# Stick-breaking attention with running products against differences of values, and subtracts and copies moved between engines, in one layer of a hybrid trunk on one Trainium2 core

## The chip, the cores and the metric

The kernel runs on one core of one Trainium2 chip. [...] The metric is the device time of one execution in microseconds (us), lower is better. Matrix products write to PSUM, eight banks of 128 partitions x 512 floats; everything else lies in SBUF.

## The reference, cut to what matters

One layer with a prompt of 2048 tokens and a sample of 32 tokens: RMSNorm, one projection, stick-breaking attention in 8 heads of 64 next to an RWKV-7 recurrence in 8 heads of 64, an output projection, and a SwiGLU block. All of it is in float32. The part that the change touches is the attention:

```python
z = jnp.einsum('bqhd,bkhd->bhqk', q, k) / math.sqrt(SB_HEAD_DIM)
mask = k_pos[None, :] < q_pos[:, None]
log_1mb = jnp.where(mask, jax.nn.log_sigmoid(-z), 0.0)
after = lax.cumsum(log_1mb, axis=3, reverse=True) - log_1mb
weight = jnp.where(mask, jnp.exp(jax.nn.log_sigmoid(z) + after), 0.0)
o = jnp.einsum('bhqk,bkhd->bqhd', weight, v)
```

So the weight of key s for query t is sigmoid(z[t,s]) times the product of sigmoid(-z[t,j]) over all keys j between s and t. With R[t,s], the product of sigmoid(-z[t,j]) over j from s up to t-1, the same weight is R[t,s+1] - R[t,s].

The recurrence keeps a 64 x 64 state per head and is done in chunks of 64 tokens (33 chunks with the sample).

## The kernel before

Products of float32 numbers are made from halves: a number is rounded to the format float32r (the upper half, "h"), the remainder is kept as the lower half ("l"), and a product is hh + hl + lh. The helper split (lines 102 to 104) makes both halves: ACT casts, then DVE, or the engine named, subtracts.

Three stages follow each other. **Projection** (superblock, to line 676): three blocks of 640, 768 and 640 tokens, in each 27 groups of 128 columns of w_in. A group is 48 matmuls on PE (colgroup, line 323), then its own work on ACT, DVE and POOL, part of it deferred by one or more groups (defer). The group "va" (g_va, lines 638 to 659) makes the attention's values for two heads: vq keeps them by columns, fin turns them to rows by token (tok_major, line 307), stores them, splits them (lines 656 and 657) and writes the halves to vhl_d in DRAM.

**Attention, recurrence, and the output projection of the first 1024 rows** run interleaved: three Python generators yield weights, and the one that is furthest behind goes next (line 1132). attention() makes two lists: A holds the scores of one block of 128 queries against up to 512 keys; B holds a turn and the values for 128 keys of such a block against up to 512 queries. In each step it gives one entry of A, one turn that is at least LAG = 4 steps behind its scores, and the values LAG2 = 2 steps after their turn. For 8 heads and 4 groups of 512 queries (qg), key blocks (kc) run from qg down to 0; kc == qg is the diagonal, where blocks are 128 to 512 wide. That makes 320 scores and 320 turns. Their steps:

- scores: two matmuls into a bank z (lines 794, 795; three banks, psZ), on the diagonal a third that adds -2^100 to the masked part (797). Then stick: ACT makes R = sigmoid(-z/8) (line 754) and b = sigmoid(z/8) (755), DVE runs the product backwards over the keys in place (757), POOL multiplies b by R shifted by one key (758). R goes on from one key block to the next; for this POOL copies or sets one column (787, 800).
- turn: up to four PE transposes of b into a bank wt (line 809; two banks, psW), and split into wth (ACT, line 103) and wtl (DVE, line 104).
- values: two matmuls that add to av (lines 823, 824), at the end of a query group ob and oT to DRAM (828 to 830).

The recurrence takes for each chunk: up (PE 1057) and its copy Us (DVE 1059), sap (PE 1067) and VS (ACT 1068), snp (PE 1076), the sum (DVE 1081) and its product with the decays PC (DVE 1083), yp (PE 1089, 1091) and Yt (ACT 1094); beside it, for the next chunk, M (DVE 1015) and TTt (ACT 1026).

**Output projection of the rest, and SwiGLU** (from line 1146) run on PE without a gap worth naming; the change does not touch them.

The order on each engine comes from the framework's scheduler, which goes through the program by priority and places an instruction where it expects its inputs and its buffer to be ready; at run time every engine keeps that order and waits by semaphores. A tile that shares a tag with others takes one of the tag's buffers and waits until it is free.

Of the kernel before, what the change touches and what calls it, by code (L numbers as in the profile page):

```python
# [17 lines left out]
P = 128  # L18
# [34 lines left out]
def kernel(ctx: ExitStack, tc: tile.TileContext, x_prompt, x_sample, cache_k, cache_v,  # L53
# [17 lines left out]
    vhl_d = [dp.tile([TP, 2, P], F32, name=f"vhl_d{c}") for c in range(4)]  # L71
    QR_d = dp.tile([NCH + 1, 4, P, P], F32, name="QR_d")
# [40 lines left out]
    with tc.tile_pool(name="pa0", bufs=1) as pe, tc.tile_pool(name="pa1", bufs=1) as pa, \  # L113
# [37 lines left out]
        R_MU, R_ST, R_W0, R_A0, R_KK, R_KA, R_RK = 0, 15, 30, 34, 38, 42, 46  # L151
# [110 lines left out]
        def superblock(sb, T0, NTILE):  # L262
# [375 lines left out]
            def g_va(w, c):  # L638
# [5 lines left out]

                def fin():
# [6 lines left out]
                    if sb == 0:  # L652
                        SP.dma_start(sv[:, c * P:(c + 1) * P], vt[0:TS, NTILE, :])
                    vs = pr.tile([P, 6, 2, P], F32R, tag="hl6", name="vs", bufs=1)
                    v4 = vt[:, 0:NTILE, :].rearrange("p j (h d) -> p j h d", d=HD)
                    ACT.copy(vs[:, 0:NTILE, :, 0:64], v4)
                    DVE.tensor_tensor(vs[:, 0:NTILE, :, 64:128], v4, f32(vs[:, 0:NTILE, :, 0:64]), ALU.subtract)
                    SP.dma_start(vhl_d[c][T0:T0 + NP].rearrange("(j t) h e -> t j h e", t=P),
                                 f32(vs[:, 0:NTILE]))
# [81 lines left out]
    with tc.tile_pool(reuse_waits="tile", name="bp", bufs=6) as bp, \  # L741
# [8 lines left out]
        NB, LAG, LAG2, RW = 10, 4, 2, PAST + TS + 1  # L750

        def stick(z, R, b, k0, n):

# [12 lines left out]
        def load(h, kc):  # L766
            k = bp.tile([P, 512], F32R, tag="k", name="k", bufs=5)
            queue(h).dma_start(f32(k), khl_d[h // 2][h % 2].rearrange("l d t -> (l d) t")[:, kc * 512:(kc + 1) * 512])
            v = bp.tile([P, 4, P], F32R, tag="vp", name="vp", bufs=5)
            queue(h).dma_start(f32(v), vhl_d[h // 2][kc * 512:(kc + 1) * 512, h % 2, :].rearrange("(j p) e -> p j e", p=P))  # L770
            pieces[h, kc] = [k, v]

        def scores(h, qg, kc, j):

            if kc == qg and j == 0:
                q = bp.tile([P, 2, 512], F32R, tag="q", name="q", bufs=3)
                cs = slice(qg * 512, (qg + 1) * 512)
                queue(h).dma_start(f32(q[:, 0]), qhl_d[h // 2][h % 2].rearrange("l d t -> (l d) t")[:, cs])
                for l in range(2):
                    queue(h).dma_start(f32(q[64 - 64 * l:128 - 64 * l, 1]), qhl_d[h // 2][h % 2, l, :, cs])  # L780
                state[h, qg] = q
            if j == 0 and (kc == qg or (qg == 2 and kc < 2)):
                load(h, kc)
# [571 lines left out]
```

## Time and profile before

| | us |
|---|---|
| median of 3 runs | 3561.26 (3555.72 to 3566.15) |
| profiled execution, its own time | 3553.88 |
| its span, first to last instruction | 3551.9 |
| projection | 0 to 911 |
| attention, recurrence, first rows | 911 to 1897 |
| rest of the output projection | 1897 to 2015 |
| SwiGLU | 2015 to 3552 |

The limits of the stages are the first matmul of scores (911.08) and the end of the last values and recurrence (about 1897). To read the page: the busy share of an engine is a mean over stages; a busy PE counts its pipeline's tail, too, so a PE at 88% is not at its peak, and the column PEld beside it is the firmer one. [...]

### The profile page before, as it was taken

Reading aid. Unit: us, or ns where it says so; the run is one execution under the profiler, and the core shown is the slowest. Engines: PE = TensorE matmul, PEld = TensorE weight load, DVE = VectorE, ACT = ScalarE, POOL = GpSimd, SP = SyncE. Lnnn points to the kernel's source line nnn. Section 1 sums busy time; section 2 is a strip of 40 time slices with the busy share of each in tenths; the row PEclk is TensorE's granted clock in tenths of the full one; section 3 lists DMA queues with packets and bytes.
Section 4 is the critical chain, followed back from the end, with each engine's and each line's share of the span. In section 5 each row is a group of like instructions: output and inputs, shape, how many; then the busy total and the mean of one; then the engine's idle time right before and its main releaser. Section 6 shows DMA issues by size and latency. Waiting matters only on the chain.

```text
span 3551.9 us, 51561 instructions
## 1 busy us (share of the span) xinstructions
PE 3348.1 (94%) x20217; PEld 2888.5 (81%) x20217; DVE 1875.3 (53%) x2437; ACT 1265.8 (36%) x2419; POOL 1299.2 (37%) x1207
## 2 busy tenths in 40 slices
PE   8999999989788889998998999999999999999998
PEld 7988898879566677776777899989998888888887
DVE  4665757668876788988884332232222412212213
ACT  6444343443444566665563321111111311111111
POOL 3322433243444576657664322211221222122121
PEclk9999999999787899998999999999999999999999
DMA  5545655566644555554554341111111511111111
GB/s 150 162 145 152 201 147 151 181 172 182 198 117 114 133 148 142 150 139 127 154 138 137 118 132 48 48 36 48 48 48 36 167 60 48 48 48 48 48 42 48
DMA packets 480362, 395.81 MB, mean 111 GB/s; under 512 B 70820, under 2 KB 402160, under 8 KB 480120
## 3 DMA queue, kind: packets, MB, share of 16 engines
q1 hardware_dynamic: 391672, 346.51, 34.1%
q10 hardware_dynamic: 88448, 46.01, 4.8%
q8 instruction: 159, 2.61, 0.3%
q14 instruction: 83, 0.68, 0.1%
HBM read 278.16 MB, written 114.28 MB: 110 GB/s over the span
## 4 chain that ended last, share of the span: by engine, by line
PE 74%; DVE 14%; issue 4%; POOL 3%; ACT 2%; DMA 2%; SPq 0%; ACTq 0%; POOLq 0%; DVEq 0%
PE gu L1268 28%; PE dn L1288 14%; PE mm L323 12%; DVE R L757 5%; PE mo L738 4%; PE wt L809 2%; DVE wtl L104 2%; DVE t L541 1%; DVE Ti L543 1%; PE av L823 1%; PE a4ps L504 1%; PE av L824 1%; PE z L794 1%; PE sap L1067 1%; PE snp L1076 1%
## 5 line engine op out<-in xcount | busy, mean ns | idle before, releaser
L758 POOL TENSOR_TENSOR b<-b,R 128x512 f32<-128x512 f32 (+2 forms) x320 | 394.4, 1238 | 271.9 <-DVE R L757 174.1
L757 DVE TENSOR_TENSOR_SCAN R<-R 128x512 f32<-128x512 f32 (+2 forms) x320 | 440.9, 1387 | 40.0 <-ACT R L754 36.8
L1291 DVE TENSOR_TENSOR x<-x,dn 128x512 f32<-128x512 f32 x374 | 255.6, 687 | 243.4 <-PE dn L1288 243.4
L1268 PE MATMUL gu<-h2h,wh 128*128 128x352 f32 (+1 forms) x1760 | 368.3, 351 | 1.7 <-ACT wh L103 1.2
L1268 PE MATMUL gu<-h2h,wl 128*128 128x352 f32 (+1 forms) x1760 | 369.0, 351 | 0.0
L1268 PE MATMUL gu<-h2l,wh 128*128 128x352 f32 (+1 forms) x1760 | 367.3, 351 | 0.0
L1268 PEld LDWEIGHTS gu<-h2h,wh 128*128 128x128 f32 x1760 | 305.0, 188 | 33.9 <-ACT wh L103 1.4
L1268 PEld LDWEIGHTS gu<-h2l,wh 128*128 128x128 f32 x1760 | 305.3, 188 | 31.0
L1268 PEld LDWEIGHTS gu<-h2h,wl 128*128 128x128 f32 x1760 | 305.1, 188 | 30.2
L1288 PE MATMUL dn<-dh,hdh 128*128 128x512 f32 x748 | 295.1, 394 | 0.0
L1288 PE MATMUL dn<-dh,hdl 128*128 128x512 f32 x748 | 295.0, 394 | 0.0
L1288 PE MATMUL dn<-dl,hdh 128*128 128x512 f32 x748 | 293.8, 393 | 0.0
L809 PE MATMUL wt<-ident,b 128*128 128x128 f32 x1088 | 203.6, 300 | 87.5 <-DVE wtl L104 67.5
L809 PEld LDWEIGHTS wt<-ident,b 128*128 128x128 f32 x1088 | 137.2, 150 | 144.1 <-DVE wtl L104 68.9
L323 PE MATMUL mm<-hh,wh 128*128 128x384 f32 (+4 forms) x1296 | 248.2, 335 | 5.8 <-DVE qhl L614 2.0
L323 PE MATMUL mm<-hh,wl 128*128 128x384 f32 (+4 forms) x1296 | 234.6, 324 | 0.0
L323 PE MATMUL mm<-hl,wh 128*128 128x384 f32 (+4 forms) x1296 | 231.9, 321 | 0.0
L754 ACT ACTIVATE R<-z 128x512 f32<-128x512 f32 (+2 forms) x320 | 174.5, 545 | 142.3 <-PE z L795 69.2
L323 PEld LDWEIGHTS mm<-hh,wh 128*128 128x128 f32 (+1 forms) x1296 | 212.7, 194 | 13.1 <-DVE qhl L614 2.3
L103 ACT CAST wth<-wt 128x512 fp32r<-128x512 f32 (+1 forms) x320 | 169.7, 533 | 135.2 <-PE wt L809 124.7
L323 PEld LDWEIGHTS mm<-hh,wl 128*128 128x128 f32 (+1 forms) x1296 | 211.2, 190 | 2.6
L104 DVE TENSOR_TENSOR wtl<-wt,wth 128x512 fp32r<-128x512 f32 (+1 forms) x320 | 188.7, 595 | 41.3 <-ACT wth L103 38.4
(752 smaller groups left out, 5899.3 us busy)
## 6 DMA issues: line engine op xcount, KB each, us to landing
wraw<-in_w_in ACTq DMA_DIRECT2D x77, 512.0 KB
rawg<-in_w_gate SPq DMA_DIRECT2D x44, 512.0 KB
rawu<-in_w_up SPq DMA_DIRECT2D x44, 512.0 KB
rawd<-in_w_down SPq DMA_DIRECT2D x44, 512.0 KB
A_d<-a SPq DMA_DIRECT2D x28, 512.0 KB
mx<-mixT_d SPq DMA_DIRECT2D x27, 512.0 KB
k<-khl_d SPq DMA_DIRECT2D x42, 256.0 KB
vp<-vhl_d SPq DMA_DIRECT2D x42, 256.0 KB
```

What stands on the lines that cost most here:

```text
L103: ACT.copy(hi, src)
L104: (eng or DVE).tensor_tensor(lo, src, f32(hi), ALU.subtract)
L323: PE.matmul(ps[0:wd, 0:s1 - s0], a_[:, kt, 0:wd], b_[:, kt, s0:s1], start=i == 0, stop=i == 3 * KT - 1)
L504: PE.matmul(ps[:, j, :], KB[64 * e:64 * e + 64, j0 + j, :], QR[64 * e:64 * e + 64, j0 + j, :], start=True, stop=True)
L738: PE.matmul(ps[0:n], a_[:, kt, 0:n], b_[:, kt, :], start=j + kt == 0, stop=j == 2 and kt == KT - 1)
L754: ACT.activation(R[:, k0:k0 + n], z[:, 0:n], AF.Sigmoid, scale=-0.125)
L757: DVE.tensor_tensor_scan(rv, rv, rv, R[:, k0 + n:k0 + n + 1], ALU.mult, ALU.bypass)
L758: POOL.tensor_tensor(b[:, 0:n], b[:, 0:n], R[:, k0 + 1:k0 + n + 1], ALU.mult)
L809: PE.transpose(pt[:, j * P:(j + 1) * P], state[h, qg, kc, j][:, kb * P:(kb + 1) * P], ident)
L1268: PE.matmul(ps[:, 0:n], a_[:, kt, :], b_[:, kt, s0:s1], start=i == 0, stop=i == 23)
L1288: PE.matmul(ps[0:n], a_[:, i * P:i * P + n], b_[:, ds_], start=k == 0, stop=k == 3 * len(js) - 1)
L1291: DVE.tensor_tensor(x1[:n, ds_], x1[:n, ds_], ps[0:n], ALU.add)
```

## The change

1. g_va makes dv, the difference of each value and the one ahead of it in time, on POOL, keeps the last column of a block for the next one in a column of cols, transposes dv on PE beside the values (line 665 of the new kernel) and splits the result out of PSUM; tiles "vs" now come from the tag r4, dv from hl6 (one buffer). The last but one value of each block of 128 tokens is split and stored, too (ve).
2. stick keeps R alone: one sigmoid, one backward product whose second operand is z in PSUM (it is bypassed) and whose start is the first column of the next key block's R. b, its multiply on POOL, and the one-column copies are gone. R is a tile of 512 in 12 buffers. The sample's scores keep the old form (s_stick).
3. values multiplies the turned R by dv. On the diagonal each 128 keys have two matmuls of their own against vd, which is dv with its last row replaced by ve; the rest of the width follows in two more.
4. In a turn with odd kb, ACT copies wt a second time (wf) and POOL subtracts, in place of DVE.
5. Loads of q, k, values and vd are issued ahead of the scores, up to LOOK = 8 steps.
6. In the recurrence ACT makes the copies M and Us, and POOL the product with PC.

```diff
@@ g_va
+                dv = pr.tile([P, 2, MX], F32, tag="hl6", name="dv", bufs=1)[:, 0]
+                pv_ = cols[:, R_PV + c:R_PV + c + 1]
+                POOL.tensor_tensor(dv[:, 0:1], pv_, vq[:, 0:1], ALU.subtract)
+                POOL.tensor_tensor(dv[:, 1:NP], vq[:, 0:NP - 1], vq[:, 1:NP], ALU.subtract)
+                ACT.copy(pv_, vq[:, NP - 1:NP])
...
-                    ACT.copy(vs[:, 0:NTILE, :, 0:64], v4)
-                    DVE.tensor_tensor(vs[:, 0:NTILE, :, 64:128], v4, f32(vs[:, 0:NTILE, :, 0:64]), ALU.subtract)
+                    for q0 in range(0, NTILE, 4):
+                        pt = psT.tile([P, 4, P], F32, tag="tr", name="pdv")
...
+                            PE.transpose(pt[:, i, :], dv[:, (q0 + i) * P:(q0 + i + 1) * P], ident)
+                        vs = r4("vs").bitcast(F32R).rearrange("p (j h e) -> p j h e", j=4, h=2)
+                        split(vs[:, 0:m, :, 0:64], vs[:, 0:m, :, 64:128],
...
+                    PE.transpose(pe_[0:NTILE, 0:P], vq[:, 0:NP].rearrange("p (j t) -> p j t", t=P)[:, :, P - 2], ident)
...
+                    SP.dma_start(ve_d[c, T0 // P:T0 // P + NTILE], f32(ve[0:NTILE]))
@@ attention
-        NB, LAG, LAG2, RW = 10, 4, 2, PAST + TS + 1
+        NB, LAG, LAG2, LOOK, RW = 12, 4, 2, 8, PAST + TS + 1
+        def stick(z, R, n, before):
+            ACT.activation(R[:, 0:n], z[:, 0:n], AF.Sigmoid, scale=-0.125)
+            rv = R[:, 0:n][:, ::-1]
+            DVE.tensor_tensor_scan(rv, rv, z[:, 0:n], before, ALU.mult, ALU.bypass)
...
+                vd = bp.tile([P, 4, P], F32R, tag="vd", name="vd", bufs=3)
+                dma(f32(vd[0:P - 1]), src[0:P - 1])
+                dma(f32(vd[P - 1:P]), ve_d[h // 2, 4 * qg:4 * qg + 4, h % 2, :].unsqueeze(0))
...
-            if kc % 2 and kc < qg:
-                POOL.tensor_copy(R[:, 1024:1025], R[:, 0:1])
-            stick(z, R, b, (kc % 2) * 512, n)
+            R = bk.tile([P, 512], F32, tag="R", name="R", bufs=NB)
+            stick(z, R, n, 1.0 if kc == qg else state[h, qg, kc + 1, j][:, 0:1])
...
-            split(wh[:, c0:], wl[:, c0:], pt[:, c0:])
+            if kb % 2:
+                wf = bq.tile([P, 512], F32, tag="wf", name="wf", bufs=3)
+                ACT.copy(wh[:, c0:], pt[:, c0:])
+                ACT.copy(wf[:, c0:], pt[:, c0:])
+                POOL.tensor_tensor(wl[:, c0:], wf[:, c0:], f32(wh[:, c0:]), ALU.subtract)
+            else:
+                split(wh[:, c0:], wl[:, c0:], pt[:, c0:])
...
+            if kc == qg:
+                vd = state[h, qg, "vd"]
+                for i, w_ in enumerate((wh, wl)):
+                    PE.matmul(av[:, c0:c0 + P], vd[:, kb, :], w_[:, c0:c0 + P], start=kb + i == 0,
+                              stop=qg == 0 and kb == 3 and i == 1)
+                c0 += P
+            if c0 < 512:
+                PE.matmul(av[:, c0:], v[:, kb, :], wh[:, c0:], start=False, stop=False)
+                PE.matmul(av[:, c0:], v[:, kb, :], wl[:, c0:], start=False, stop=kc == 0 and kb == 3)
@@ recurrence
-                DVE.tensor_copy(M[96:128], mp[96:128, 0:256].rearrange("p (h t) -> p h t", h=H))
+                ACT.copy(M[96:128], mp[96:128, 0:256].rearrange("p (h t) -> p h t", h=H))
-                DVE.tensor_copy(Us[up_], up[up_])
+                ACT.copy(Us[up_], up[up_])
-                DVE.tensor_tensor(s3, s3, PC[up_, ch, :].unsqueeze(2).to_broadcast([64, H, 64]), ALU.mult)
+                POOL.tensor_tensor(s3, s3, PC[up_, ch, :].unsqueeze(2).to_broadcast([64, H, 64]), ALU.mult)
```

What this does to the order shows at three places. The first is PE in the projection's second block, behind the transposes of the values of group va; mm are the next group's products, pdv the transposes of the differences, pve that of ve. Before:

```order
L495 MATMUL ptk<-ident,KB 128x128 x4
L504 MATMUL a4ps<-QR,KB 128x128 x8
L307 MATMUL ptok<-ident,vq 128x128 x6
L323 MATMUL mm<-hh_3003,wh 128x384 x8
L323 MATMUL mm<-hh_3003,wl 128x384 x8
```

Now, on the same engine at the same place:

```order
L308 MATMUL ptok<-ident,vq 128x128 x6
L665 MATMUL pdv<-ident,dv 128x128 x4
L324 MATMUL mm<-hh_3071,wh 128x384
L665 MATMUL pdv<-ident,dv 128x128 x2
L324 MATMUL mm<-hh_3071,wh 128x384
L673 MATMUL pve<-ident,vq 6x128
L324 MATMUL mm<-hh_3071,wh 128x384 x6
```

Seven transposes have come in between the values' own and the next group's products, two of those products among them. The second place is DVE in the middle of the attention; R is the backward product, wtl the lower half of a turned block, VST the recurrence's state. Before:

```order
L757 SCALAR_TENSOR_TENSOR R<-R 128x512
L104 TENSOR_TENSOR wtl<-wt,wth 128x512
L757 SCALAR_TENSOR_TENSOR R<-R 128x512
L1081 TENSOR_TENSOR VST<-snp,VST 64x512
L104 TENSOR_TENSOR wtl<-wt,wth 128x512
L1083 TENSOR_TENSOR VST<-VST,PC 64x512
L757 SCALAR_TENSOR_TENSOR R<-R 128x512
```

Now, on DVE in the same stretch of work:

```order
L105 TENSOR_TENSOR wtl<-wt,wth 128x512
L774 SCALAR_TENSOR_TENSOR R<-R,z 128x512 x2
L105 TENSOR_TENSOR wtl<-wt,wth 128x512
L774 SCALAR_TENSOR_TENSOR R<-R,z 128x512 x2
L105 TENSOR_TENSOR wtl<-wt,wth 128x512
L774 SCALAR_TENSOR_TENSOR R<-R,z 128x512
L1123 TENSOR_TENSOR VST<-snp,VST 64x512
```

One subtract now stands to two backward products, which read z, and the product with PC has left. The third place is POOL in the attention; b is the weight that was multiplied there. Before:

```order
L758 TENSOR_TENSOR b<-b,R 128x384
L758 TENSOR_TENSOR b<-b,R 128x512 x2
L800 COPY R<-R 128x1
L758 TENSOR_TENSOR b<-b,R 128x512
L800 COPY R<-R 128x1
```

Now, on POOL; mx is the lower half of an input of the output projection:

```order
L843 TENSOR_TENSOR wtl<-wf,wth 128x512 x2
L1033 MEMSET TTt 32x512
L843 TENSOR_TENSOR wtl<-wf,wth 128x512
L1125 TENSOR_TENSOR VST<-VST,PC 64x512
L843 TENSOR_TENSOR wtl<-wf,wth 128x512
L743 TENSOR_TENSOR mx<-mx,mh 128x1024
```

The multiplies ahead of the transposes are gone; in their place stand subtracts behind every second turn, and the recurrence's product, between POOL's other work.

## Rows read from the trace of the kernel before

**Rows 1.** Stages: length, then busy us of PE, PEld, DVE, ACT, POOL; clock, DMA.

```profile
core 0: us, PE busy (x) PEld busy (x) DVE busy (x) ACT busy (x) POOL busy (x), PEclk, DMA share, GB/s
911.00:1250.00 339.00, 274.48 (x1949) 216.98 (x1949) 246.20 (x325) 169.32 (x384) 178.58 (x213) 0.78 0.50 133
...
1550.00:1897.00 347.00, 318.82 (x2615) 251.89 (x2614) 297.87 (x321) 205.90 (x408) 230.08 (x216) 0.97 0.51 134
911.00:1897.00 986.00, 868.80 (x6862) 689.92 (x6863) 806.69 (x935) 561.22 (x1167) 608.19 (x635) 0.90 0.52 136
0.00:911.00 911.00, 842.13 (x5241) 786.50 (x5241) 614.23 (x879) 388.37 (x779) 299.96 (x290) 0.96 0.58 167
...
2015.00:3552.00 1537.00, 1525.48 (x7596) 1324.67 (x7596) 417.31 (x575) 281.87 (x424) 346.89 (x248) 1.00 0.20 62
```

**Rows 2.** Chain of waits from 911 to 1897 us, shares by line.

```profile
by line: DVE R L757 16.7%; issue 8.4%; PE wt L809 8.2%; DVE wtl L104 5.8%; PE mo L738 5.5%; PE av L823 4.7%; PE av L824 4.3%; PE z L794 3.9%; PE sap L1067 3.5%; PE snp L1076 3.2%; PE z L795 3.0%; POOL b L758 2.7%; PE up L1057 2.1%; PE yp L1
```

**Rows 3.** Groups, 911 to 1897 us: busy us, mean ns, idle before by releaser.

```profile
L757 DVE TENSOR_TENSOR_SCAN R<-R 128x512 f32<-128x512 f32 x224 | 356.9, 1599 | 21.4 <-ACT R L754 19.3 <-POOL R L800 0.3
L758 POOL TENSOR_TENSOR b<-b,R 128x512 f32<-128x512 f32 x224 | 296.4, 1328 | 176.5 <-DVE R L757 116.2 <-ACT b L755 17.7 <-ACT R L754 11.8
L809 PE MATMUL wt<-ident,b 128*128 128x128 f32 x1088 | 203.6, 300 | 87.5 <-DVE wtl L104 67.5 <-POOL b L758 19.1
L104 DVE TENSOR_TENSOR wtl<-wt,wth 128x512 fp32r<-128x512 f32 x224 | 150.6, 677 | 35.2 <-ACT wth L103 33.1
L754 ACT ACTIVATE R<-z 128x512 f32<-128x512 f32 x224 | 137.2, 613 | 93.2 <-PE z L795 69.2 <-PE z L797 14.4 <-POOL b L758 6.8
...
L755 ACT ACTIVATE b<-z 128x512 f32<-128x512 f32 x224 | 136.8, 611 | 2.3 <-PE wt L809 2.2
L103 ACT CAST wth<-wt 128x512 fp32r<-128x512 f32 x224 | 133.3, 598 | 101.6 <-PE wt L809 91.3 <-DMA k<-khl_d 7.2 <-DVE VST L1081 2.2
...
L794 PE MATMUL z<-k,q 128*128 128x512 f32 x224 | 102.4, 457 | 7.2 <-ACT b L755 5.9 <-DMA k<-khl_d 1.3
...
L1083 DVE TENSOR_TENSOR VST<-VST,PC 64x512 f32<-64x512 f32 x31 | 35.7, 1151 | 1.0
...
L1059 DVE COPY Us<-up 64x512 f32<-64x512 f32 x33 | 22.9, 695 | 9.3 <-PE up L1057 8.3
L951 POOL TENSOR_TENSOR Yt<-Yt,gl 128x512 f32<-128x512 f32 x15 | 22.9, 1527 | 2.9 <-DVE Yt L949 1.7 <-ACT b L755 0.9
...
L1015 DVE COPY M<-mps 32x256 f32<-32x256 f32 x32 | 13.8, 430 | 10.5 <-PE mps L1013 9.6
```

**Rows 4.** Single lines, 911 to 1897 us: duration ns min/median/max, first and last start.

```profile
L757 DVE TENSOR_TENSOR_SCAN R<-R x320: 446/1284/3324, 921.3 to 1880.6; 128x512 f32<-128x512 f32 x96, 128x128 f32<-128x128 f32 x32, 128x384 f32<-128x384 f32 x32
...
L104 DVE TENSOR_TENSOR wtl<-wt,wth x320: 258/660/694, 932.8 to 1891.8; 128x512 fp32r<-128x512 f32 x128, 128x256 fp32r<-128x256 f32 x32
...
L1083 DVE TENSOR_TENSOR VST<-VST,PC x31: 689/803/2908, 1049.8 to 1874.8; 64x512 f32<-64x512 f32 x31
```

**Rows 5.** PE in order of time, end of the projection: start us, us, instructions.

```profile
840.71 1.55 PE L323 MATMUL mm<-hh,wh 128*128 128x384 f32 x8
842.11 1.55 PE L323 MATMUL mm<-hh,wl 128*128 128x384 f32 x8
...
852.15 0.71 PE L307 MATMUL ptok<-ident,qf 128*128 128x128 f32 x5
852.61 1.20 PE L323 MATMUL mm<-hh,wh 128*128 128x256 f32 x8
```

**Rows 6.** Groups, 0 to 911 us, columns as in rows 3.

```profile
L344 POOL TENSOR_TENSOR df<-xp 128x640 f32<-128x640 f32 x14 | 18.8, 1340 | 35.4 <-ACT xp L335 31.3 <-ACT kbt L497 2.7 <-DVE rr L346 1.4
...
L307 PE MATMUL ptok<-ident,vq 128*128 128x128 f32 x64 | 11.8, 321 | 1.6 <-DVE kt__8881 L309 1.6
...
L657 DVE TENSOR_TENSOR vs<-vt,vs 128x768 fp32r<-128x768 f32 x4 | 6.0, 1512 | 1.8 <-ACT vs L656 1.8
...
L656 ACT CAST vs<-vt 128x640 fp32r<-128x640 f32 x7 | 5.1, 730 | 14.1 <-DVE vt L309 10.1 <-DMA qhl_d<-qhl 2.2 <-DMA A_d<-a 1.8
```

More of the change, by code (lines that the diff above doesn't have):

```diff
@@ L764, in queue, with load @@
             return ACT if h == 0 else SP
[L766 to L775, printed above, removed]
+        def load(h, qg, kc):
+            dma = queue(h).dma_start
+            if kc == qg:
@@ L776, in scores @@
                 q = bp.tile([P, 2, 512], F32R, tag="q", name="q", bufs=3)
                 cs = slice(qg * 512, (qg + 1) * 512)
-                queue(h).dma_start(f32(q[:, 0]), qhl_d[h // 2][h % 2].rearrange("l d t -> (l d) t")[:, cs])
+                dma(f32(q[:, 0]), qhl_d[h // 2][h % 2].rearrange("l d t -> (l d) t")[:, cs])
                 for l in range(2):
-                    queue(h).dma_start(f32(q[64 - 64 * l:128 - 64 * l, 1]), qhl_d[h // 2][h % 2, l, :, cs])
+                    dma(f32(q[64 - 64 * l:128 - 64 * l, 1]), qhl_d[h // 2][h % 2, l, :, cs])
@@ L781, in scores @@
                 state[h, qg] = q
-            if j == 0 and (kc == qg or (qg == 2 and kc < 2)):
-                load(h, kc)
-            if kc == qg:
-                R = bk.tile([P, RW], F32, tag="R", name="R")
-                e = (qg % 2) * 512 + (j + 1) * P
-                POOL.memset(R[:, e:e + 1], 1.0)
-                state[h, qg, "R", j] = R
-            R = state[h, qg, "R", j]
+            if kc < qg and not (qg == 2 and kc < 2):
+                return
+            k = bp.tile([P, 512], F32R, tag="k", name="k", bufs=6)
@@ new lines, in load @@
+            dma(f32(k), khl_d[h // 2][h % 2].rearrange("l d t -> (l d) t")[:, kc * 512:(kc + 1) * 512])
+            src = vhl_d[h // 2][kc * 512:(kc + 1) * 512, h % 2, :].rearrange("(j p) e -> p j e", p=P)
+            v = bp.tile([P, 4, P], F32R, tag="vp", name="vp", bufs=6)
+            dma(f32(v), src)
+            pieces[h, kc] = [k, v]
+            if kc == qg:
+                vd = bp.tile([P, 4, P], F32R, tag="vd", name="vd", bufs=3)
+                dma(f32(vd[0:P - 1]), src[0:P - 1])
+                dma(f32(vd[P - 1:P]), ve_d[h // 2, 4 * qg:4 * qg + 4, h % 2, :].unsqueeze(0))
+                state[h, qg, "vd"] = vd
@@ L790, in scores @@
+        def scores(h, qg, kc, j):
             k = pieces[h, kc][0]
@@ L822, in values @@
             av = state[h, qg, "o"]
-            PE.matmul(av[:, c0:], v[:, kb, :], wh[:, c0:], start=kc == qg and kb == 0, stop=False)
-            PE.matmul(av[:, c0:], v[:, kb, :], wl[:, c0:], start=False, stop=kc == 0 and kb == 3)
+            if kc == qg:
+                vd = state[h, qg, "vd"]
[6 more added lines that the diff above has]
+                PE.matmul(av[:, c0:], v[:, kb, :], wl[:, c0:], start=False, stop=kc == 0 and kb == 3)
             if kc == 0 and kb == 3:
@@ L894, in attention @@
         def attention():
-            A, B = [], []
+            A, B, loads = [], [], []
             for hq, h in [(hq, h) for hq in range(2) for h in range(H)]:
@@ L905, in attention @@
                     for kc in range(qg, -1, -1):
+                        loads.append((len(A), h, qg, kc))
                         for j in range(4):
@@ L916, in attention @@
                 w = 0.0
+                while loads and loads[0][0] <= t + LOOK:
+                    load(*loads.pop(0)[1:])
                 if t < len(A):
```

27 lines of the change are left out of this document (16 added, 11 removed).

## The prediction

> **What bounds the kernel now.** I read the stages first [rows 1]. SwiGLU has PE busy for 1525 of 1537 us at full clock; nothing of the change is there. In the projection PE is busy for 842 of 911 us: every matmul added there costs its own time. The middle stage, 911 to 1897 us, is another matter. PE shows 869 of 986 us, but its weight loads, the firmer column, only 690 (70%), while DVE has 807 (82%; 86% in the last third), POOL 608 and ACT 561. So in this stage DVE is nearest to its limit, and PE has room that it can't use, because each block goes PE, ACT, DVE, POOL, PE, ACT, DVE, PE in lists of fixed order. The chain of waits says the same [rows 2]: the backward product (L757) is the largest line, 16.7%, wtl has 5.8%, POOL's multiply 2.7%. And the groups show where PE stands still [rows 3]: ahead of its transposes 67.5 us for wtl and 19.1 us for POOL's b.
>
> The single lines then show something that the means hide [rows 4]. The backward product takes 1284 ns in its median over all widths, and up to 3324; its mean at 512 wide is 1599 [rows 3]. The decay product (L1083) goes from 689 to 2908. Both read two operands from SBUF. wtl, which reads one from PSUM and one from SBUF, stays between 258 and 694. So a DVE instruction of the first kind is drawn out in this stage and one of the second is not, and the change makes the product of the second kind, with z from PSUM.
>
> **The change, part by part.** Sums are against the profiled execution's 3553.9 us; the median of the runs lies 7.4 us above it, which I add at the end. The stage's chain is 986 us, so 1% is 9.9 us.
>
> *POOL's multiply and the second sigmoid go.* On the chain the multiply is 2.7%, 27 us: **-27**. ACT's b ran beside other work; 137 us of ACT's list are free at 512 wide [rows 3], and what takes their place is below.
>
> *The backward product reads z.* There is no row of a product with a PSUM operand. Its ends: as long as now (1599), or undisturbed (1284 at 512 wide; that this is the 512 value follows from 512 being 224 of the 320). wtl against L1083 [rows 4] makes the lower end the nearer one. The line's 16.7% are 165 us, and 1 - 1284/1599 is 20%: **-32**, with 0 as the other end. [...]
>
> *Half of wtl leaves DVE.* 160 of 320 turns. Of the chain's 5.8%, 57 us, half: **-28**. For these turns the bank wt is freed by ACT's second copy (as the cast, 598 ns) in place of DVE's subtract (677), so PE's transposes wait no longer than for the other half, unless ACT is behind. ACT loses about 170 us of b over all widths (137 at 512, 96 narrower ones at less) and takes 160 copies, at most 96, plus Us and M, some 37 [rows 3]: its list gets shorter.
>
> *Us, M and the product with PC leave DVE*: 22.9 + 13.8 + 35.7 = 72 us of its list [rows 3]. DVE's two large lines have 22.5% of the chain (222 us) for 545 or so of its 807 busy us; at that ratio, rounded down to 0.28 because these wait for PE as well, 72 us are **-20**. Ends 0 and -72. POOL's product is bounded by L951, 1527 ns at twice the partitions, against 1151: 0.4 us more in each of 31 chunks, 12 us, beside attention work that fills PE; taken at nothing, 12 as the other end.
>
> *TensorE's clock.* In 911 to 1250 us the mean granted clock is 0.78, against 0.97 in the last third [rows 1]; in that first part PE has 64 us idle, more than twice the share of idle that the last third has. Less waiting there should give some of it back. If PE paced it throughout, 274 x (1 - 0.78/0.97) = 54 us; I take **-12**, about a quarter, with ends 0 and -54.
>
> *PE's additions in the stage.* 192 more matmuls: on the diagonal kb 0 to 2 have four in place of two, 6 x 32 groups. The columns are the same. A transpose of 128 columns follows the next in (852.61 - 852.15)/5 = 92 ns, and a product of 384 columns in (842.11 - 840.71)/8 = 175 ns [rows 5], so 128 of its columns cost 58; the cut costs 92 - 58 = 34 ns each, with the weight load: 7, taken as **+8**; at most 192 x 92 = 18.
>
> *Projection.* 64 transposes of dv at 92 ns are 6 us, 12 of ve 1 to 3. The banks that they take are evacuated by ACT and DVE, which have work of the next group ahead; PE's waits for such a bank are 1.6 us for 64 now [rows 6]. dv has one buffer, shared with the q and k halves, so the group q's ACT cast waits behind va's transposes, and the evacuations behind that cast in ACT's list with it; as a price, the 2.2 and 1.8 us that ACT waited for buffers at L656. Together **+12**, from 4 to 30. POOL's subtract (as L344, 1340 ns, 12 times) stands ahead of the next group's df, which waits for ACT anyway (31 of 35 us); cover gone, 16 us. ACT and DVE split the same width from PSUM as they did from SBUF, where L657 took up to 1512: nothing.
>
> *New waits.* A bank z is now held until DVE's product has read it, not until the second sigmoid: 613 + 1284 against 613 + 611 ns, and DVE's queue. What is behind it is PE's next score, and all of PE's list. Three banks, and a score every 986/320 = 3.1 us: a bank has 9 us, the chain needs 2.5. Taken at nothing; the price is a rival. Loads stand up to eight steps ahead in SP's list, where one that waits for its buffer holds up the recurrence's loads behind it; scores wait 1.3 us for a load today, so neither gain nor loss is counted.
>
> Sum: -27 -32 -28 -20 -12 +8 +12 = -99. 3553.9 - 99 + 7.4 = **3462 us**.
>
> **The rivals.**
>
> *PE paces the stage.* After the change no other engine is near its limit: DVE loses 87 (wtl; 65 of them at 512) + 71 (224 x 0.315) + 72 and comes to about 577 of 986, POOL and ACT to less. PE's loads are then the most, 690 + 12. If they reach the 0.82 that DVE holds today, the stage is 702/0.82 = 856 us, a gain of 130; with the first part's loads at the later clock (217 x (1 - 0.78/0.97) = 43 less) it is 804, a gain of 182. The middle, 156, less 12 for the projection: 3417. For it speaks that the lists get shorter on three engines at once; against it, that a chain through five lists seldom lets the next engine go as far.
>
> *The z banks.* The 67.5 us that PE waits for wtl today come back as waits for z: -99 + 67 = -32, 3529. It decides once DVE is more than 6 us behind its sigmoids; POOL's waits for the product, 116 us in all, show that DVE does fall behind.
>
> *POOL in the path of the values, slower than before.* In odd turns the lower half is ready after 598 + 598 + 1328, not 598 + 677: 1.25 us later in 96 turns, half of that in 64, 160 us. If PE stands for all of it, -99 + 160 = +61: 3622. It decides where PE's list reaches the values sooner than 2.5 us behind the turn, or POOL is that much behind; two steps are 6 us, which speaks against it, and on POOL the mx subtract and the recurrence's product stand between, which speaks for it. [...]
>
> *The product isn't shorter from PSUM*, so that this part doesn't do what it might: -67, 3494; with a product of more than 1599, less.
>
> **How the numbers follow.** The forecast, 3435 to 3490: 0.52. PE paces, 3417: 0.25. z banks, 3529: 0.12. POOL in the path: 0.06. Product not shorter: 0.05. The forecast is the likeliest. The range runs from 3390, most of the way to the 182 of the first rival, to 3535, above the z banks; it leaves out a fifth of the first rival, a third of the second and the third. About 0.3% is what a measurement of this kernel can tell from no change. Faster by more than that: everything but POOL's case and a part of the z banks, 0.91; within it 0.04, slower 0.05.
>
> **What would show it.** In the profile after: the middle stage at 870 to 910 us; DVE at about 65% of it; the product at 512 wide near 1284 ns with hardly a spread, like wtl; PE's waits for wtl about halved and none on POOL ahead of a transpose; mm's stage 4 to 30 us longer; the recurrence no later. The forecast is wrong if PE's scores wait for z's banks (DVE's product as the releaser), if values wait for POOL's wtl, if the product stays at 1599, or if the projection loses more than 30 us. If PE is over 80% in weight loads, the first rival has it.

## The result, and the profile of the changed kernel

The changed kernel takes **3707.9 us** (median of 4, 3700.4 to 3713.7), the kernel before 3563.7 (median of 4): 1.041 times as long, 95% interval 1.038 to 1.043. The forecast was 3462, with 3390 to 3535 as its range. It was wrong, and on the wrong side: +144 instead of -99. The prediction had given any slowing a chance of 0.05.

The stages of the changed kernel, to be held against [rows 1]: length; busy us, with counts, of PE (matrix products), PEld (their weight loads), DVE (scans and elementwise work), ACT (sigmoids, casts, copies) and POOL (elementwise work); granted clock, the share of its full speed that PE had in the stretch; DMA share; GB/s.

```profile
core 0: us, PE busy (x) PEld busy (x) DVE busy (x) ACT busy (x) POOL busy (x), PEclk, DMA share, GB/s
0.00:911.00 911.00, 847.26 (x5192) 788.20 (x5192) 602.29 (x852) 389.42 (x801) 312.13 (x300) 0.94 0.55 160
911.00:1410.00 499.00, 328.55 (x2365) 273.45 (x2365) 217.17 (x316) 173.64 (x387) 95.51 (x107) 0.72 0.43 117
1410.00:2060.00 650.00, 589.70 (x4845) 477.09 (x4845) 370.94 (x419) 358.67 (x702) 270.41 (x227) 0.95 0.55 141
2060.00:3705.00 1645.00, 1631.29 (x8089) 1407.32 (x8089) 449.53 (x617) 314.49 (x471) 387.53 (x279) 1.00 0.21 66
```

The loss is in the middle stage. The last product of the values starts at 2046 us instead of 1892, and in the first part, to 1410 us, every engine is idle much of the time, PE for 170 of 499 us, at a granted clock of 0.72. DVE, the fullest engine of the stage before, has 588 us here for 807. So work did leave DVE, and something else came to set the pace. The chain of waits, 940 to 1990 us, shares by line, says what (compare [rows 2]):

```profile
by line: SPq L813 14.2%; DMA vd<-vhl_d 7.5%; PE wt L835 5.7%; PE mo L756 5.3%; DMA ABc<-A_d 4.7%; ACTq L813 4.4%; PE z L822 4.2%; PE z L823 3.3%; DMA mx<-mixT_d 2.9%; issue 2.8%; PE av L862 2.7%; PE av L863 2.7%; PE snp L1118 2.6%; PE sap L
```

SPq and ACTq are the lists of SP and ACT while they issue DMAs. The scan, 16.7% before, isn't among the lines that the row has room for. In its place stand the issue of line 813, the load of the single row into vd, and ahead of it the load of vd's other 127 rows (L812), with its wait. The issues themselves, as ns minimum/median/maximum and first and last start:

```profile
L812 SPq DMA_DIRECT2D vd<-vhl_d x28: 239/362/425, 975.6 to 1966.3; - x28
L812 ACTq DMA_DIRECT2D vd<-vhl_d x4: 246/495/785, 953.3 to 1332.4; - x4
L813 SPq DMA_DIRECT2D vd<-ve_d x28: 618/12686/24127, 975.9 to 1967.0; - x28
L813 ACTq DMA_DIRECT2D vd<-ve_d x4: 12933/16497/20235, 954.7 to 1333.7; - x4
```

The 127 rows are issued in 0.36 us; the DMA behind them stands 12.7 us in the list in its median. It isn't slow by itself: its minimum is 618 ns, in the one of its 28 issues on SP ahead of which other DMAs had come in between, and then the first of those stood, for 10.07 us. SP's list in order of time (start us, duration us), once as it mostly goes and once with another DMA next:

```profile
1150.58 0.25 SPq L812 DMA_DIRECT2D vd<-vhl_d  x1
1150.88 12.51 SPq L813 DMA_DIRECT2D vd<-ve_d  x1
1163.43 0.47 SPq L1027 DMA_DIRECT2D ABc<-A_d  x1
...
1377.22 0.36 SPq L812 DMA_DIRECT2D vd<-vhl_d  x1
1379.98 10.07 SPq L1022 DMA_DIRECT2D QAc<-QR_d  x1
...
1392.81 0.62 SPq L813 DMA_DIRECT2D vd<-ve_d  x1
```

What the DMA engines do meanwhile is in 40 slices of 0.75 us from 1150 us on (busy tenths, then GB/s):

```profile
DMA  9996200000000000000389820237658996101001
GB/s 313 195 234 126 60 18 21 20 21 20 20 21 20 20 21 20 20 21 23 102 294 208 148 40 22 32 82 150 202 137 281 243 289 193 36 22 44 22 22 33
```

Ahead of and behind the load the engines move up to 313 GB/s, during it a steady 20, with the mean busy share of the 16 engines under a tenth (0.07 from 1155 to 1162 us; 16 x 0.07 = 1.1, about one engine's time). The load has 127 x 4 x 512 = 260,096 bytes; at 20.5 GB/s that is 12.7 us, the median of the row above. So these rows go at about a tenth of the rate around them, and SP issues nothing until they are nearly through. Behind it stand the recurrence's loads (ABc, QAc, TTt) and the attention's next ones; on ACT's list, which holds four of these loads, the sigmoids stand behind it too: the first one starts at 995.6 us, behind two such issues of 13.6 and 20.2 us.

Why such a load goes at one engine's share, 20 GB/s, isn't shown: the trace doesn't say which engine moves what. That the following issue stands is shown by the rows of L813.

The groups that answer to [rows 3], 911 to 2050 us (busy us, mean ns, idle before by releaser):

```profile
L774 DVE TENSOR_TENSOR_SCAN R<-R,z 128x512 f32<-128x512 f32 x224 | 280.9, 1263 | 167.7 <-ACT R L772 167.0
L835 PE MATMUL wt<-ident,R 128*128 128x128 f32 x1088 | 197.6, 295 | 21.4 <-DVE wtl L105 19.9 <-ACT wf L842 1.3
L843 POOL TENSOR_TENSOR wtl<-wf,wth 128x512 fp32r<-128x512 f32 x96 | 124.2, 1294 | 214.8 <-ACT wf L842 198.6 <-PE z L825 3.8 <-issue 3.7
L822 PE MATMUL z<-k,q 128*128 128x512 f32 x224 | 106.8, 477 | 61.4 <-DVE R L774 61.4
L1101 ACT COPY Us<-up 64x512 f32<-64x512 f32 x33 | 19.2, 582 | 43.5 <-PE up L1099 43.2
```

Two of the steps are there as forecast: the scan at 512 wide is 1263 ns for 1599, and PE waits 21.4 us ahead of its transposes where it waited 87.5. And one that was taken at nothing: PE's scores wait 61 us for a bank z that the scan still holds.

### The profile page after: what moved, and what is told of

It is laid out like the page before. It is cut to its first block, busy times and chain, and to the rows that moved or that the text cites. A ratio compares the mean times of both kernels' runs of the same rounds, so it can differ in the third digit from the quotient of the medians.

```text
span 3705.9 us, 51315 instructions
## 1 busy us (share of the span) xinstructions
PE 3396.8 (92%) x20485; PEld 2946.1 (79%) x20485; DVE 1639.9 (44%) x2203; ACT 1236.2 (33%) x2360; POOL 1065.6 (29%) x912
## 4 chain that ended last, share of the span: by engine, by line
PE 66%; DMA 9%; DVE 8%; SPq 6%; issue 4%; POOL 3%; ACT 2%; ACTq 1%; POOLq 0%; DVEq 0%
PE gu L1310 27%; PE dn L1330 14%; PE mm L324 7%; PE mo L756 4%; SPq L813 4%; DMA vd<-vhl_d 2%; PE wt L835 2%; DMA ABc<-A_d 1%; DVE t L542 1%; PE z L822 1%; ACTq L813 1%; DVE Ti L544 1%; DMA mx<-mixT_d 1%; PE z L823 1%; DMA wraw<-in_w_in 1%
## 5 line engine op out<-in xcount | busy, mean ns | idle before, releaser
L774 DVE TENSOR_TENSOR_SCAN R<-R,z 128x512 f32<-128x512 f32 (+2 forms) x320 | 344.8, 1088 | 264.6 <-ACT R L772 263.0
L843 POOL TENSOR_TENSOR wtl<-wf,wth 128x512 fp32r<-128x512 f32 (+2 forms) x160 | 171.5, 1073 | 414.2 <-ACT wf L842 357.0
L835 PE MATMUL wt<-ident,R 128*128 128x128 f32 x1088 | 197.6, 295 | 21.4 <-DVE wtl L105 19.9
L822 PE MATMUL z<-k,q 128*128 128x512 f32 (+2 forms) x320 | 143.0, 447 | 79.9 <-DVE R L774 61.8
L324 PEld LDWEIGHTS mm<-hl,wh 128*128 128x128 f32 (+1 forms) x1296 | 209.4, 188 | 2.6
L104 ACT CAST dh<-rawd 128x1024 fp32r<-128x1024 f32 x44 | 44.2, 1047 | 425.5 <-PE dn L1330 424.4
```

The source lines that it names most:

```text
L104: ACT.copy(hi, src)
L324: PE.matmul(ps[0:wd, 0:s1 - s0], a_[:, kt, 0:wd], b_[:, kt, s0:s1], start=i == 0, stop=i == 3 * KT - 1)
L774: DVE.tensor_tensor_scan(rv, rv, z[:, 0:n], before, ALU.mult, ALU.bypass)
L822: PE.matmul(z[:, 0:n], state[h, qg][:, 0, js], k[:, 0:n], start=True, stop=False)
L835: PE.transpose(pt[:, j * P:(j + 1) * P], state[h, qg, kc, j][:, kb * P:(kb + 1) * P], ident)
L843: POOL.tensor_tensor(wl[:, c0:], wf[:, c0:], f32(wh[:, c0:]), ALU.subtract)
```

## The experiments

Theories: **the load** (127 rows at about one engine's share, 20 GB/s, hold what stands behind them in SP's and ACT's lists), against **a slow load of one row**, and, for what is left, **the terms of the sum**. All edits are small; each time is the median, with the ratio to the kernel before and its 95% interval. The kernels were run in several sets, each with its own runs of the kernel before, whose medians lie between 3555.5 and 3567.5 us; a difference of two kernels from different sets is uncertain by some 10 us for that.

**112 + 15 rows instead of 127.** The changed kernel, one line different:

```diff
-                dma(f32(vd[0:P - 1]), src[0:P - 1])
+                dma(f32(vd[0:112]), src[0:112])
+                dma(f32(vd[112:P - 1]), src[112:P - 1])
```

> The changed kernel with one edit: vd's load of 127 rows is issued as 112 rows and 15 rows; the load of the last row (ve) is as it was. Theory A (the load of 127 rows is moved by so few DMA engines that the next DMA on its queue can't be issued for some 13 us, and SP's and ACT's lists stand): the issue after it, L813 in the profile of the changed kernel (median 12.7 us), falls under 1.5 us, the lines SPq, ACTq L813 and DMA vd leave the chain of waits, and the time falls by 150 to 260 us, to 3450 to 3560, near the 3462 forecast. Theory B (the one-row load from ve_d is slow by itself): its issue stays above 10 us and the time within 20 us of 3708. Theory C (loads ahead of the scores hold up the recurrence's loads whatever their rows): the time falls by less than 60 us.

3552.9 us, 1.0004 (0.9985 to 1.0022): 155 us less than the changed kernel (148 when each is held against the kernel before of its own set), for the same bytes in one DMA more. The issues of the three DMAs (112, 15 and 1 rows):

```profile
L812 SPq DMA_DIRECT2D vd<-vhl_d x28: 310/474/1482, 964.6 to 1818.5; - x28
L813 SPq DMA_DIRECT2D vd<-vhl_d x28: 337/498/771, 965.5 to 1819.0; - x28
L814 SPq DMA_DIRECT2D vd<-ve_d x28: 617/626/660, 966.6 to 1819.6; - x28
```

The load of one row, unchanged, is never over 0.66 us now. So the 127 rows are the cause of the loss against before, and the slow single row falls. But the time is that of the kernel before, and 91 us above the forecast: the gain is missing, too.

**The load alone, in the kernel before.** A load of vd that nothing reads, once with 127 + 1 rows, once with 112 + 15 + 1, both from vhl_d:

```diff
+            if kc == qg:
+                vd = bp.tile([P, 4, P], F32R, tag="vd", name="vd", bufs=2)
+                src = vhl_d[h // 2][kc * 512:(kc + 1) * 512, h % 2, :].rearrange("(j p) e -> p j e", p=P)
+                queue(h).dma_start(f32(vd[0:P - 1]), src[0:P - 1])
+                queue(h).dma_start(f32(vd[P - 1:P]), src[P - 1:P])
```

> The kernel before with dead loads added and nothing else: for each of the 32 diagonal blocks a tile vd is loaded in 127 rows and one row, both from vhl_d, in two buffers, and nothing reads it. Theory A: the issue behind each 127-row load takes 10 us or more, and the kernel before gets slower by 80 to 250 us, to 3640 to 3810, though no engine computes anything more. Theory B (ve_d's load) and theory C (the loads' lead): within 30 us of 3563.

> The same dead loads in the kernel before, with the 127 rows issued as 112 and 15; the bytes are the same and there is one issue more. Theory A: no issue above 2 us, the time within 25 us of 3563. If it is the bytes or the number of DMAs that cost, it is as slow as with 127 rows.

127 rows: 3766.4, 1.0599 (1.0573 to 1.0625), and the issue behind the load shows the same picture:

```profile
L776 SPq DMA_DIRECT2D vd<-vhl_d x28: 622/12614/16837, 963.2 to 2029.2; - x28
```

112 rows: 3672.4, 1.0344 (1.0311 to 1.0378). The step from 127 to 112 + 15 is worth 94 us here. But I had expected hardly any cost for what remains, and it is 116 us: loads that nothing reads, of 8 MB in all, aren't free in this stage. Two more kernels ask which part of them it is, with all 128 rows in one DMA, and in two of 112 and 16:

```diff
-                queue(h).dma_start(f32(vd[0:P - 1]), src[0:P - 1])
-                queue(h).dma_start(f32(vd[P - 1:P]), src[P - 1:P])
+                queue(h).dma_start(f32(vd), src)
```

> The kernel before, with a load that nothing reads: all 128 rows of the tile of the diagonal, in one DMA, where 112 + 15 + 1 rows in three cost 116 us and 127 + 1 in two cost 210. Theory 1 (the bytes, 8 MB in the two stretches, delay the loads that the kernel waits for): 3640 to 3680 again. Theory 2 (the small loads of 15 rows and of one row, or the time to issue three, made it): 3556 to 3590.

> The kernel before with the dead load in two DMAs, of 112 and of 16 rows, and none of one row. One DMA of 128 rows cost 31 us, three of 112, 15 and 1 rows 116. Theory 1 (each DMA more costs about the same, by its issue and its small pieces): 3625 to 3645. [...]

One DMA: 3592.0, 1.0090 (1.0071 to 1.0108), 31 us. Two: 3646.7, 1.0243 (1.0208 to 1.0279), 79 us. So one whole load costs about 31, and each further DMA costs more than its own half microsecond of issue in 32 places. What goes with it in the traces is POOL: ahead of clearing a part of TTt, a tile of the recurrence, it waits for the product sap for 27.7 us before, 48.4 with one DMA, 63.0 with two, 98.9 with three, and PE waits for POOL's b ahead of its transposes 19.1, 37.7, 50.0 and 71.4. That fits a recurrence whose loads come later, and a list of POOL in which b stands behind TTt; it is read from the waits and not shown by an experiment. The granted clock of the stretch from 911 to 1890 us goes down beside it, 0.90, 0.90, 0.88 and 0.86; what that costs was not measured.

**No second copy.** With R = 1 at each masked key, the value that row 127 of vd carried can be added once for each block: vp with all its rows in the place of vd, and one product of a row of ones with the block's last value.

```diff
-                dma(f32(vd[0:P - 1]), src[0:P - 1])
-                dma(f32(vd[P - 1:P]), ve_d[h // 2, 4 * qg:4 * qg + 4, h % 2, :].unsqueeze(0))
+                dma(f32(ve), ve_d[h // 2, 4 * qg:4 * qg + 4, h % 2, :].unsqueeze(0))
...
+            PE.matmul(av[:, c0:], v[:, kb, :], wh[:, c0:], start=kc == qg and kb == 0, stop=False)
+            if kc == qg:
+                PE.matmul(av[:, c0:c0 + P], state[h, qg, "ve"][0:1, kb, :], oner, start=False, stop=False)
+            PE.matmul(av[:, c0:], v[:, kb, :], wl[:, c0:], start=False, stop=kc == 0 and kb == 3)
```

> The changed kernel without the second copy of the differences: the diagonal blocks use the tile vp with all its rows, and the last value of each block, which the 127 rows left room for, is added by a product of one row of ones with a tile of one row (4 x 128), 128 columns wide, one per diagonal block. So no load of 127, 112 or 15 rows is left, 8 MB less is loaded, and one small product takes the place of one of two. With 112 + 15 rows the changed kernel took 3553, as the kernel before. Theory 1 (the load of the second copy eats what the rest of the change gains; as dead work beside the kernel before it cost 116): 3430 to 3480. Theory 2 (the rest of the change gains nothing, because TensorE paces the stage and new waits take the place of the old ones; the second copy is hidden once its rows are many enough): 3535 to 3560.

3510.5, 0.9858 (0.9838 to 0.9879): faster than before by 51 us, outside what either theory gave, half of the forecast's gain. Against the kernel with 112 + 15 rows it is 42 us. The tile ve now holds each block's last value, not the last but one.

**Which part of those 42 us.** The copy's loads back as dead loads, with two and with three buffers for ve, and, apart from that, the products in the changed kernel's pieces:

```diff
+                vd = bp.tile([P, 4, P], F32R, tag="vd", name="vd", bufs=2)
+                dma(f32(vd[0:112]), src[0:112])
+                dma(f32(vd[112:P - 1]), src[112:P - 1])
```

```diff
-            PE.matmul(av[:, c0:], v[:, kb, :], wh[:, c0:], start=kc == qg and kb == 0, stop=False)
+            if kc == qg:
+                for i, w_ in enumerate((wh, wl)):
+                    PE.matmul(av[:, c0:c0 + P], v[:, kb, :], w_[:, c0:c0 + P], start=kb + i == 0, stop=False)
```

> e5_no_vd (3510) with the second copy's loads back, in 112 and 15 rows, which nothing reads; its products stay as in e5_no_vd. Theory 1 (of the 42 us between the changed kernel with 112 + 15 rows and e5_no_vd the loads are the cause, by their bytes and by what stands behind them on the lists): 3540 to 3560. Theory 2 (the products in more pieces are the cause): 3505 to 3522.

> e11_dead_loads (3596) with three buffers for ve, as e5_no_vd (3510) has, in place of two. In e11_dead_loads SyncE's list stood 42.8 us in five waits for the products that read an older ve, which neither e5_no_vd nor the changed kernel has. Theory 1 (those waits are in the 85, and the loads alone cost what the changed kernel with 112 + 15 rows loses by them): 3535 to 3560. Theory 2 (the loads alone cost 85, and the changed kernel with 112 + 15 rows hides part of it): 3580 to 3600.

> e5_no_vd (3510) with each diagonal product in the two pieces of the changed kernel, both from vp; no second copy is loaded. There are 192 products more, which the forecast put at 8 us, and at 24 if all stood on the path. Theory 1 (loads): 3508 to 3525. Theory 2 (pieces): 3535 to 3555.

Dead loads: 3595.7, 1.0109 (1.0088 to 1.0130), of which a part was my own doing. With two buffers for ve, SP's list stood at its load (L819) for products that read an older one (us in total, times, longest):

```profile
SPq L819 <- PE av L864: 42.8, 5, 19.8
```

With three buffers that row is down to 10.2 us in three waits (9.2 without the loads, so the expectation was wrong that they have none), and the time is 3583.3, 1.0088 (1.0070 to 1.0106), in the range of the second theory: the loads alone cost 73 us, at 112 + 15 rows still. Pieces: 3529.0, 0.9936 (0.9912 to 0.9960), 18 us, between the ranges of the two theories. By each set's own kernel before the two are 78 and 24. Together 91, more than 42; but the kernel without the copy has 128 small products with ones that the kernel with 112 + 15 rows lacks, and they have 41.8 us of PE's time (327 ns each). 73 + 18 - 42 is 49, near the 42. That they cost all of their busy time is an assumption: no run has taken them out alone.

**The terms of the sum.** First the scan: the kernel with 112 + 15 rows, and the scan's second operand in SBUF again, which also lets the bank z go after the sigmoid.

```diff
-            DVE.tensor_tensor_scan(rv, rv, z[:, 0:n], before, ALU.mult, ALU.bypass)
+            DVE.tensor_tensor_scan(rv, rv, rv, before, ALU.mult, ALU.bypass)
```

> As the run with 112 and 15 rows, and the backward product's bypassed second operand is R itself in SBUF again, not z in PSUM, so that z's bank is free after the sigmoid. If the forecast's term for the product is right (an operand in PSUM keeps POOL's work out of it), the product at 512 wide grows from 1.2 to 1.3 us toward 1.4 to 1.6 us, by POOL's share of now, and the time by 5 to 30 us over the run with 112 and 15 rows. If the banks z that wait for the product cost more than that (PE's scores waited 61.8 us for it in the changed kernel), the time falls by 10 to 50 us.

3598.3, 1.0131 (1.0104 to 1.0158): 45 us slower than with z, more than the 5 to 30 expected. Its groups, and below them the same two with z:

```profile
L774 DVE TENSOR_TENSOR_SCAN R<-R 128x512 f32<-128x512 f32 x224 | 331.6, 1500 | 56.1 <-ACT R L772 55.2
L1126 POOL TENSOR_TENSOR VST<-VST,PC 64x512 f32<-64x512 f32 x31 | 50.4, 1625 | 56.9 <-DVE VST L1124 35.1 <-issue 10.6 <-PE wt L836 4.1
...
L774 DVE TENSOR_TENSOR_SCAN R<-R,z 128x512 f32<-128x512 f32 x224 | 278.6, 1261 | 78.9 <-ACT R L772 78.1
L1126 POOL TENSOR_TENSOR VST<-VST,PC 64x512 f32<-64x512 f32 x31 | 32.3, 1041 | 57.5 <-DVE VST L1124 36.3 <-issue 10.6 <-PE z L826 4.8
```

1500 ns for 1261, and POOL's product with PC 1625 for 1041: as means, instructions of both engines took longer here, where DVE's scan reads both operands from SBUF. Most of their instructions are hardly slower, some much: over all widths the scan has 393/1269/3407 ns as minimum, median and maximum (384/1256/1283 with z), and POOL's product 1039/1159/5287 (1039/1041/1045 with z).

Then, on the kernel without the copy, the lower half of the weights on DVE for every turn, and separately the recurrence's two copies and its product with PC on DVE, as before:

```diff
-            if kb % 2:
-                wf = bq.tile([P, 512], F32, tag="wf", name="wf", bufs=3)
...
-            else:
-                split(wh[:, c0:], wl[:, c0:], pt[:, c0:])
+            split(wh[:, c0:], wl[:, c0:], pt[:, c0:])
```

```diff
-                ACT.copy(Us[up_], up[up_])
+                DVE.tensor_copy(Us[up_], up[up_])
...
-                POOL.tensor_tensor(s3, s3, PC[up_, ch, :].unsqueeze(2).to_broadcast([64, H, 64]), ALU.mult)
+                DVE.tensor_tensor(s3, s3, PC[up_, ch, :].unsqueeze(2).to_broadcast([64, H, 64]), ALU.mult)
```

> As e5_no_vd, but the lower half of the weights is made on VectorE for every turn, as in the kernel before (no tile wf, no subtraction on GpSimd). Theory 1 (the forecast's term of 28 us for the half that left VectorE): 15 to 40 slower than e5_no_vd. Theory 2 (GpSimd's 1.07 us for a tile, after two copies on ScalarE, stands in the path of the values and gives the gain back): from 5 slower to 40 faster than e5_no_vd.

> As e5_no_vd, but the recurrence's two copies (Us and M) and its product with PC are on VectorE, as in the kernel before. Theory 1 (the forecast's term of 20 us for what left VectorE): 10 to 30 slower than e5_no_vd. Theory 2 (the recurrence is a chain of steps that nothing else waits for, VectorE has time to spare, and the product is quicker there): within 10 of e5_no_vd, or faster.

Split on DVE: **3495.7**, 0.9818 (0.9800 to 0.9837), 15 us faster than with half of it on ACT and POOL, and the fastest version of all. Recurrence on DVE: 3514.0, 0.9869 (0.9844 to 0.9894), no difference from 3510.5. The groups of the fastest, 940 to 1850 us:

```profile
L778 DVE TENSOR_TENSOR_SCAN R<-R,z 128x512 f32<-128x512 f32 x224 | 283.0, 1264 | 76.0 <-ACT R L776 75.4
L838 PE MATMUL wt<-ident,R 128*128 128x128 f32 x1088 | 189.4, 284 | 10.8 <-DVE wtl L105 10.3
L105 DVE TENSOR_TENSOR wtl<-wt,wth 128x512 fp32r<-128x512 f32 x224 | 150.5, 673 | 45.6 <-ACT wth L104 45.0
L825 PE MATMUL z<-k,q 128*128 128x512 f32 x224 | 98.9, 441 | 6.8 <-DVE R L778 6.8
```

With all of wtl on DVE, PE waits for it 10.3 us, where it was 67.5 before [rows 3]; with half on POOL it is 8.8, and the values wait 5.7 for POOL's half (8.1 in the weight loads). There was nothing left for the split to gain.

**The start of the stage.** In the fastest version the first values come at 970.6 us and the last at 1832.8; before 933.2 and 1891.9. The stage is 96 us shorter and starts 37 later. Three attempts on the start: ve of the projection in a ring of its own, no loads ahead, and the first with the loads ahead only from the second step.

```diff
-                    ve = pr.tile([P, 256], F32, tag="t2", name="ve").bitcast(F32R).rearrange("p (h e) -> p h e", h=2)
+                    ve = r4("ve")[:, 0:256].bitcast(F32R).rearrange("p (h e) -> p h e", h=2)
...
-        NB, LAG, LAG2, LOOK, RW = 12, 4, 2, 8, PAST + TS + 1
+        NB, LAG, LAG2, LOOK, RW = 12, 4, 2, 0, PAST + TS + 1
...
-                while loads and loads[0][0] <= t + LOOK:
+                while loads and loads[0][0] <= t + (LOOK if t else 0):
```

> As e6_split_dve (3496), but the tile ve of the projection's end lies in the ring r4 and no longer in the buffer t2, which the inverse on VectorE uses step by step. In e6_split_dve the last ve waited 7.9 us for that inverse, ScalarE's list of loads stood behind it, and the first values came 37 us later than in the kernel before (970 against 933). Theory 1 (that wait holds the start): 3483 to 3492. Theory 2 (the start is held by the projection's longer end and by the loads ahead, which keep the DMA engines 0.8 to 0.9 busy from 930 to 990): within 4 of e6_split_dve.

> As e6_split_dve (3496), but without the eight steps ahead (LOOK 0): a load is issued at the step that uses it, as in the kernel before. Theory 1 (the loads ahead crowd the start): 5 to 15 faster, the first values at 950 to 960. Theory 2 (loads ahead spare TensorE waits later, and the start is held by the projection's end): 5 to 40 slower.

> As e8_ve_r4, and the eight steps ahead begin only behind the first step, so that the first loads stand alone. If each of the two holds the start: 3470 to 3487, the first values at 940 to 955. If the projection's longer end holds it: within 5 of e6_split_dve (3496).

3497.1, 3501.4 and 3498.6 (0.9816, 0.9828, 0.9821): none gains, and the first values come later, at 982.8, 976.8 and 988.3 us. The first edit has only exchanged one wait for another: ACT's cast of ve waited 9.2 us for the inverse, and in the new ring it waits 10.0 us for the store of vs (in the third version, too). So it doesn't tell whether that wait holds the start. The loads ahead don't hold it: without them the first values are no earlier. And a late start isn't paid one for one: in the first of the three the first values come 12 us later than in the fastest version, the last ones at 1833.3 for 1832.8, and the time is the same. What holds the start, beyond the projection's end (its last products start at 927.3 for 908.1 before), stays open.

## Why the prediction was wrong, step by step

**The step that failed: the loads.** The forecast's paragraph on new waits says of the loads that "neither gain nor loss is counted", and weighs only one that waits for its buffer. It never prices vd's own two DMAs, although they are in the diff: 32 loads of 127 rows. They were put at nothing without a row, and as no row of before showed such a load, both ends had to be wide. The runs put some 150 us on the 127 rows (155, or 148 by each set's own kernel before), because what stands behind them on SP's and ACT's lists waits 10 to 24 us each time, and 73 on the copy's loads even in 112 + 15 rows. The first alone turns the sign. It was no rival either: the range ended at 3535.

**POOL's multiply and the scan, -27 and -32.** Right in mechanism. The multiply's share was not measured alone. The scan at 512 is 1263 ns, at the lower end taken (1284), with hardly a spread, 385/1260/1284 over all widths where [rows 4] has 446/1284/3324. Putting it back costs 45 us in a kernel whose POOL does other work, so 32 was rather low. What drew it out before, no row of before says; the run that puts it back has both engines slower, as means: 1500 ns for the scan and 1625 for POOL's product with PC where the scan reads SBUF alone, 1261 and 1041 where it reads z.

**Half of wtl, -28.** Wrong in sign: it costs 15. The share of the chain was real before the change, but the other parts had already taken it: DVE, busy for 594 of 986 us without the copy, no longer holds wt's banks (PE waits 8.8 us for wtl there, 67.5 before). The first rival, that PE paces the stage, comes nearest to what is left: in the fastest version PE is busy for 931 and loads weights for 737 of the same 986 us, and of its chain from 911 to 1890 us the largest lines are PE's, with the scan at 4.9% for 16.7. But 737 is 75%, under the 80% that the prediction asked for as its sign, and no run takes work from PE alone, so this is a reading and not shown.

```profile
by line: PE mo L756 11.7%; PE wt L838 10.2%; PE av L855 7.0%; PE z L825 6.3%; PE av L852 5.4%; PE z L826 5.3%; DVE R L778 4.9%; PE snp L1110 3.8%; PE yp L1123 3.7%; PE sap L1101 3.6%; PE yp L1125 3.6%; issue 3.2%; DVE wtl L105 3.2%; PE up L
...
911.00:1897.00 986.00, 930.57 (x7341) 736.79 (x7340) 660.89 (x907) 483.63 (x944) 218.30 (x187) 0.95 0.57 152
```

**Us, M and the product with PC, -20.** Nothing, by the same token (3514.0 against 3510.5). The ratio behind it was misread, too: DVE's two large lines have 630 us over all widths, not 545, which makes it 0.35 and not 0.41; it was rounded to 0.28 in any case.

**These two shares were priced as if each stood alone.** Without them the sum is -99 + 28 + 20 = -51, which would be 3510; the kernel that has neither the second copy nor the split on POOL has 3496. That is no test of the sum, for this kernel also has the small products with ones.

**The clock, -12.** It came with the rest, as far as it can be told: 0.95 over the stage for 0.90 [rows 1] in the fastest version; the changed kernel, with PE idle at the start, has 0.72 to 1410 us. Its own worth was not measured.

**PE's pieces, +8**, at most 18: 18 measured (24 by the set's own kernel before), so it was sized low. **The projection, +12**, from 4 to 30: 20 by its last product, and the first values another 16 later in the kernel without the copy.

**The z banks, taken at nothing.** PE waits 61 us for them in the changed kernel, 22 with 112 + 15 rows, 6.6 without the copy and 6.8 in the fastest. Waits (us in total, times, longest) of ACT and PE in the changed kernel, and of PE with 112 + 15 rows:

```profile
ACT L772 <- issue: 43.1, 1, 43.1
PE z L822 <- DVE R L774: 61.8, 11, 36.4
...
PE z L823 <- DVE R L774: 21.9, 19, 9.5
```

Two of PE's waits in the changed kernel, 36.4 and 13.3 us, lie where ACT's list stands behind loads of vd (to 994 and to 1307 us), so that the scan has nothing to work on. So most of the 61 us, and of the rival's 67, came from ACT's and SP's lists standing still, not from the bank's longer hold; three banks were enough where the loads didn't stall (6.6 and 6.8 us of waits). **POOL in the path of the values** was given 3622 and 0.06; it exists, at 15 us and not 160.

The middle stage was to be 870 to 910 us, 76 to 116 less than its 986. From the first product of the values to the last, 959 before, it is 1041 in the changed kernel, 874 without the copy, 862 in the fastest: 85 and 96 less, so the size that was forecast for this stage came out once the copy was gone. That is in part luck: the scan's share seems to have been worth more than was forecast, half of wtl and the recurrence's copies nothing or less.

## What to carry to other kernels

Price each new DMA before anything else, by the rate and the issue times that a trace shows for a load of its shape, and with everything that stands behind it in its queue's list: here 127 rows went at 20 GB/s and the next issue stood 12.7 us in its median, and 112 and 15 rows took half a microsecond of issue each. The row less than 128 cost some 150 us, more than the 99 that the forecast had the whole change save; with the odd row added by another way the kernel took 3510.5 us for 3707.9. And when several edits each take a share of the same chain, price the second with the first already done, and ask after each which engine paces now.

## What the runs showed that I had not expected

- Behind a load of 127 rows x 4 pieces of 512 bytes the next DMA of the same list stands 12.7 us in its median on SP and 16.5 on ACT. Where both lists have such a load at once it is longer: 24.1 us on SP from 975.9 us beside 20.2 on ACT from 974.0, and 23.0 from 1288.3 beside 19.4 from 1287.5. The two loads don't add their rates: from 979 to 997 us the DMA engines move 21 GB/s at a mean busy share of 0.07, as with one such load. In 112 + 15 rows both are issued in about half a microsecond each. The engines in 40 slices of 0.75 us from 970 us on:

```profile
DMA  6679346999200000000000000000000000000100
GB/s 184 189 191 309 123 150 188 322 356 282 59 22 22 22 21 21 21 20 20 21 20 20 21 20 20 21 20 20 21 20 21 20 20 23 20 20 21 42 20 21
```

- Loads that nothing reads cost 31 us in one DMA of 128 rows, 79 in two and 116 in three (32 times each, 256 KB), in a stage whose DMA engines are busy for 0.55, 0.53 and 0.51 of it (911 to 1890 us; 0.52 before, to 1897). The mechanism is open.
- A product with one row of ones, 128 columns wide, occupies PE for 322 ns in its median in the trace, no less than one of full depth (306 and 276 for vd's two, in the changed kernel).
